# Four weight splits per LayerNorm moved from GpSimd to VectorE, and a constants step put on the background list

## Chip, cores, metric

One Trainium2 chip, one core. The metric is the device time of one launch in microseconds (us), the median of several runs; a profiled execution of the same program gives the trace.

## The reference, cut to what matters

Two layers of a trunk run over 640 tokens: a context part of 128 and a latent part of 512 tokens, 1024 features wide, in float32. Layer 0 has an even mixer (a gated MLP and pooling groups) and a convolutional feed-forward part; layer 1 has an odd mixer (a gated linear recurrence and latent attention) and another feed-forward part. Around each of the four sub-layers stand the same steps:

```python
sh1, sc1, g1, sh2, sc2, g2 = split(silu(c) @ w_mod[l] + b_mod[l], 6)   # one set for each of the two parts
h = x * (1 + sc) + sh
x = layernorm(ALPHA * x + g * sublayer(h)) * ln_g + ln_b
# feed-forward: z = dwconv3(h @ w_up); sublayer = (silu(z_gate) * z_value) @ w_down
# odd mixer, constants: -RG_C * softplus(-lam) for the decay of the recurrence
```

So w_mod (2 x 1024 x 6144) has to be multiplied by two vectors, once for each layer, and the gate g2 of layer 0 is needed when the first feed-forward's results are added up.

## The kernel before

**Products.** Each float32 product is made of three: a weight or an activation is split in a rounded part `hi` and a rest `lo`, and `mm3` (L150 to L155) runs hi x hi, hi x lo and lo x hi on TensorE. A weight's split (`split`, L96) is a cast on ScalarE (L98) and a subtraction (L101) on GpSimd or VectorE; `want` lists the weights in order of use with the engine for the subtraction (GpSimd where none is named). `load` (L115) issues a weight's DMA from SyncE into one of 4 raw buffers `r`, `prep` (L121) splits it into a pair of the 12 buffers `w`, `pump` (L136) keeps some weights loaded and split ahead, `take` hands one out.

**Order.** A scheduler orders the instructions of the engines by their place in the program and by modelled times; `high_priority` moves a split forward. `keep_in_program_order` pins an instruction behind the one that its engine was given just before in the program. The instructions of SyncE, that is all DMA issues, stay exactly in the order in which the program writes them.

**Sub-layers.** The 640 tokens are five tiles of 128 rows (`ys`). `project` (L474) makes the output product tile by tile in two halves of 512 columns, each in one of 4 PSUM buffers `B`; `accumulate` (L465) multiplies a half by the gate (L468, VectorE) and adds it to `ys` (L470 GpSimd, or L472 VectorE). In the last projection of a sub-layer `Norm` runs along: `stats` (mean, variance, L382 normalizes), `affine` (L403: scale L410, shift L413, of tiles 0 to 3), a shorter way for tile 4 (L370, then `second`, L392), and `turn` (L418), which transposes a normalized tile (L427) and splits it (L98, L101) into the next sub-layer's input. `project` ends with `turn(3)` and `turn(4)`, between them the first products of the next sub-layer (`nxt.start`), and sets `pin`, so that the next split alone is pinned.

**Feed-forward.** `ffn` goes over 22 column blocks p, each with a gate and a value product of 48 matmuls (PSUM buffers `A`, 2), a convolution (L527 ScalarE, L528 and L529 VectorE), and a product L538. They are grouped in pieces of 4, 4, 4, 3, 3 and 4 blocks (`PIECES`); after a piece is made, the piece before it is projected (`down`, which calls `project`).

**Background list.** `back` holds generators; `tick` runs the first one to its next `yield`, and the loops call it once or twice per product. `drain(k)` runs ticks until only k entries are left on the list. `mod_vec` (L250) is the modulation: for each of the 8 blocks of each of the vectors asked for it loads 512 KB of w_mod into a buffer `r` (L237, always one ahead) and multiplies it by the two vectors `cb` (L243, two VectorE instructions); after some vectors `rows_out` (L204) transposes the result on TensorE (L211), copies it (L213) and stores it to DRAM (`scr`, L215). `mod_bc` (L313) loads such rows back, spread over the partitions (L310).

After the even mixer the list holds the previous norm's `lazy` (L432), one vector of layer 0 (8 blocks) and five of layer 1 (40 blocks), written at the end as

```python
back.append(mod_vec(0, (5,), cb))
back.append(mod_vec(1, (0, 1, 2, 3, 4), cb))
rg_consts()
```

and in the feed-forward's `up`, after block p = 7, stands

```python
if p == PIECES[2] - 1:
    drain(1)
    gate.extend(mod_bc(l, SG2))
```

`rg_consts` (L934, through `softplus_neg`, L906) makes the odd mixer's constants with about 35 small VectorE instructions and one ScalarE instruction, from `vec`, which is loaded at the start.

Of the kernel before, what the change touches and what calls it, by code (L numbers as in the profile page):

```python
# [14 lines left out]
ALU = mybir.AluOpType  # L15
# [25 lines left out]
def tile_hybrid_trunk(ctx, tc, xT, x, vecs, tabs, wm0, wm1, wmT, crow, grow, lnrow, bs, w_u, w_v, w_p, w_s, w_pool, w_eo,  # L41
# [4 lines left out]
    dve, act, pe, pool, sp = nc.vector, nc.scalar, nc.tensor, nc.gpsimd, nc.sync  # L46
# [22 lines left out]
    def W(shape, dt=F32):  # L69
        return wpool.tile(shape, dt, tag="w", name=nm("w"))  # L70
# [4 lines left out]
    def Tm(shape, dt=F32):  # L75
        return tpool.tile(shape, dt, tag="t", name=nm("t"))

    def M(shape, dt=F32):
        return mpool.tile(shape, dt, tag="m", name=nm("m"))
# [10 lines left out]
    def B():  # L90
        return psB.tile([128, 512], F32, tag="B", name=nm("B"))
# [4 lines left out]
    def split(hi, lo, src, hi_eng, lo_eng):  # L96
        if hi_eng is act:
            act.copy(hi, src)  # L98
        else:
            hi_eng.tensor_copy(hi, src)  # L100
        return lo_eng.tensor_tensor(lo, src, f(hi), ALU.subtract)  # L101

# [1 line left out]
    queue = []  # L104
    ready = []
    loaded = []
    hold = [2]
    depth = [2]
    pin = [False]
    urgent = [True]  # L110

    def want(src, shape, scale=None, lo=None):
# [2 lines left out]
    def load():  # L115
        src, shape, scale, lo = queue.pop(0)
        raw = R(shape)
        sp.dma_start(raw, src)
        loaded.append((raw, shape, scale, lo))

    def prep(lo_eng=None):  # L121
        if not loaded:
            load()
        raw, shape, scale, lo_ = loaded.pop(0)
        lo_eng = lo_eng or lo_
        if scale is not None:
            dve.tensor_scalar(raw, raw, scale, ATTN_SCALE, ALU.mult, ALU.mult)
        hi, lo = W(shape, F32R), W(shape, F32R)
        with tc.high_priority() if urgent[0] else ExitStack():
            i = split(hi, lo, raw, act, lo_eng or pool)  # L130
        if pin[0]:
            tc.keep_in_program_order(i)
            pin[0] = False
        ready.append((hi, lo))

    def pump():  # L136
# [13 lines left out]
    def mm3(out, terms):  # L150
        n = len(terms)
        for i, (ah, al, bh, bl) in enumerate(terms):
            pe.matmul(out, ah, bh, start=i == 0, stop=False)  # L153
            pe.matmul(out, ah, bl, start=False, stop=False)  # L154
            pe.matmul(out, al, bh, start=False, stop=i == n - 1)  # L155
# [4 lines left out]
        pool.tensor_tensor(r, v, eps[:, 2:3], ALU.pow)  # L160
        return r

# [1 line left out]
    back = []  # L164

    def tick(n=1):
        for _ in range(n):
            while back:
                try:
                    next(back[0])  # L170
                    break
                except StopIteration:
                    back.pop(0)
# [2 lines left out]
        while len(back) > k:  # L176
            tick()

# [1 line left out]
    vec = cpool.tile([128, V_N], F32, name="vec")  # L180
    sp.dma_start(vec, vecs)
    ident = cpool.tile([128, 128], F32, name="ident")
# [9 lines left out]
    scr = [[dpool.tile([2, D], F32, name=f"scr{l}_{i}") for i in range(6)] for l in range(2)]  # L192
    SA1, SB1, SG1, SA2, SB2, SG2 = range(6)

# [1 line left out]
    def lnc(l, j):  # L196
        o = V_LN + (l * 4 + j) * 8
        return vec[:, o:o + 8].unsqueeze(1).to_broadcast([128, 2, 8])
# [117 lines left out]
    def ln_row(l, j):  # L316
        return bc_load(lnrow[:, (l * 4 + j) * D:(l * 4 + j + 1) * D])

# [1 line left out]
    def new_h():  # L320
        hi = [S([128, 2, T], F32R) for _ in range(4)]
        lo = [S([128, 2, T], F32R) for _ in range(4)]
        return hi, lo
# [14 lines left out]
        group(u, h, out, 0)  # L338
        group(u, h, out, 1)

# [1 line left out]
    ys = [None] * 5  # L342

    class Norm:
# [58 lines left out]
        def affine(self, i):  # L403
            y = ys[i]
            a, b = self.rows(i)
            ht = [Tm([128, 512]), Tm([128, 512])]
            for half in range(2):
                sl = slice(half * 512, half * 512 + 512)
                on_dve = half or self.nxt is None
                op = (dve if on_dve else pool).tensor_tensor(ht[half], y[:, sl], a[:, sl], ALU.mult)  # L410
                if on_dve:
                    tc.keep_in_program_order(op)
                (dve if half and (i == 3 or self.nxt is None or i == 0) else pool).tensor_tensor(ht[half], ht[half], b[:, sl], ALU.add)  # L413
                if self.nxt is None:
                    sp.dma_start(o_y[i][:, sl], ht[half])
            self.ht[i] = ht
# [42 lines left out]
    def settle():  # L459
        if pending[0] is not None:  # L460
            for _ in pending[0]:
                pass
            pending[0] = None
# [10 lines left out]
    def project(src, ks, wu, gate, norm=None, nxt=None, mid=None, ticks=1):  # L474
        settle()
        for i in range(5):
            c = slice(TOK[i], TOK[i] + 128)
            sums = None if norm is None else [M([128, 1]), M([128, 1])]
            for half in range(2):
                sl = slice(half * 512, half * 512 + 512)  # L480
                ps = B()
                mm3(ps, [(src[0][k // 2][:, k % 2, c], src[1][k // 2][:, k % 2, c], wu[n][0][:, sl], wu[n][1][:, sl])
                         for n, k in enumerate(ks)])
                accumulate(i, half, ps, gate, sums)
                if norm is not None and half == 0 and i and norm.fast(i - 1):
                    norm.second(i - 1)
            if mid is not None:
                mid(i)
            if norm is None:
                tick(ticks)  # L490
            else:
                norm.stats(i, sums, (lambda: norm.turn(i - 2)) if norm.nxt is not None and i >= 2 else None)
        if nxt is not None:
            next(nxt)
            norm.turn(3)
            next(nxt)
            norm.turn(4)
            pin[0] = True

# [1 line left out]
    def ffn(l, h):  # L501
        def plan():
            prev = None
# [124 lines left out]
                residual(norm)  # L628
        return nxt

# [1 line left out]
    def even_first(cb):  # L632
        want(w_v[0], [128, 2, 512])
        want(w_u[0], [128, D])
# [85 lines left out]
        for e in (dve, pool, dve):  # L720
            prep(e)
# [180 lines left out]
        nxt = out_proj(w_eo, ycat, gate, make_norm, nxt_sub, lambda i: pool_out(3, qs[3]) if i == 2 else None)  # L902
        return nxt, cb

# [1 line left out]
    def softplus_neg(lam):  # L906
        n = 8
        t, u, e, z, z2, s = (M([128, n]) for _ in range(6))
        dve.tensor_scalar(t, lam, -1.0, None, ALU.mult)
        dve.tensor_tensor(u, t, lam, ALU.max)  # L910
        act.activation(u, u, AF.Tanh, scale=1.0 / 32.0)
        dve.tensor_scalar(e, u, 1.0, None, ALU.add)
        dve.reciprocal(e, e)
        dve.tensor_scalar(u, u, -1.0, 1.0, ALU.mult, ALU.add)
        dve.tensor_tensor(e, e, u, ALU.mult)
        for _ in range(4):
            dve.tensor_tensor(e, e, e, ALU.mult)
        dve.tensor_scalar(z, e, 2.0, None, ALU.add)
        dve.reciprocal(z, z)
        dve.tensor_tensor(z, z, e, ALU.mult)  # L920
        dve.tensor_tensor(z2, z, z, ALU.mult)
        dve.tensor_scalar(s, z2, 1.0 / 17.0, 1.0 / 15.0, ALU.mult, ALU.add)
        for c in (13, 11, 9, 7, 5, 3, 1):
            dve.tensor_tensor(s, s, z2, ALU.mult)
            dve.tensor_scalar(s, s, 1.0 / c, None, ALU.add)
        dve.tensor_tensor(s, s, z, ALU.mult)
        dve.tensor_scalar(t, t, 0.0, None, ALU.max)
        dve.scalar_tensor_tensor(s, s, 2.0, t, ALU.mult, ALU.add)
        return s
# [2 lines left out]
    hb = cpool.tile([128, 16], F32, name="hb")  # L932

    def rg_consts():  # L934
        s = softplus_neg(vec[:, V_LAM:V_LAM + 8])
        dve.tensor_scalar(rg[:, 0:8], s, -2.0, None, ALU.mult)
        dve.tensor_scalar(rg[:, 8:16], s, -4.0, None, ALU.mult)
        dve.tensor_scalar(hb, vec[:, V_BA:V_BA + 16], 0.5, None, ALU.mult)

    def odd_mixer(h):  # L940
# [98 lines left out]
        def rest(make_norm, nxt_sub):  # L1039
# [166 lines left out]
                qt.append(q)  # L1206
            uk = take()

            # attention: heads in pairs
            kts = [[[W([96, 896], F32R) for _ in range(2)] for _ in range(1 + hh)] for hh in range(2)]  # L1210
            for kt, e in zip(kts[0] + kts[1], ((dve, act), (dve, act), (dve, act))):
                for q in range(2):
# [96 lines left out]
            for n in range(len(steps) + 3):  # L1309
                if n < len(steps):  # L1310
                    j, hh, i = steps[n]
# [23 lines left out]
                if n >= 3:  # L1335
                    j, hh, i = steps[n - 3]
# [29 lines left out]
        eng.tensor_tensor(x1, a, b, ALU.subtract)  # L1366
        eng.tensor_tensor(x2, c, e, ALU.add)

# [1 line left out]
    def sub(maker, *args):  # L1370
        return lambda h: Sub(*maker(*args, h))

    nxt, cb = even_mixer(lambda: Norm(0, 0, (0, SA2)), sub(ffn, 0))
    back.append(mod_vec(0, (5,), cb))
    back.append(mod_vec(1, (0, 1, 2, 3, 4), cb))
    rg_consts()
    nxt = nxt.rest(lambda: Norm(0, 2, (1, SA1)), sub(odd_mixer))
    nxt = nxt.rest(lambda: Norm(1, 0, (1, SA2)), sub(ffn, 1))
    cb = [V([128, D]) for _ in range(2)]
# [119 lines left out]
```

## Time and profile before

| | |
|---|---|
| time, median of 3 runs | 1579.65 us (1574.54 to 1591.32) |
| span of the profiled execution | 1581.2 us |
| TensorE busy in it | 1473.5 us (93%) |
| VectorE, GpSimd, ScalarE busy | 1002.7, 785.0 and 585.9 us |
| mean granted TensorE clock | 0.976 |

The times are those of the launch; of the profiled execution the span from its first to its last instruction is given, and no other time of its own. The span stands 1.6 us above the median and inside the three runs. Busy times of different engines lie beside each other; TensorE's idle time is what an improvement elsewhere can take away.

### The profile page before, as it was taken

To read this page: it belongs to the slowest core of one execution; us is meant where nothing else is said; L and a number is where in the kernel's file an instruction comes from. 1 tells how busy PE (TensorE), PEld (TensorE's weight loads), DVE (VectorE), ACT (ScalarE), POOL (GpSimd) and SP (SyncE) were. 2 spreads that over 40 slices of the span, in tenths; PEclk is the share of its full clock that TensorE was granted. 3 is DMA by queue.
4 is the path that set the end of the run, shared out by engine and by line. 5 is a ranking of instruction groups with operands and counts; after the bars stand their busy time and mean duration, and the time that the engine had idled before them with its cause. 6 is when DMAs were issued, how large, how long until landed. Compare 5 with 4: busy or idle time off the path is not lost. (4 is left out here: it accounts for less than half of the span.)

```text
span 1581.2 us, 21997 instructions
## 1 busy us (share of the span) xinstructions
PE 1473.5 (93%) x8741; PEld 1320.6 (84%) x8741; DVE 1002.7 (63%) x1432; ACT 585.9 (37%) x868; POOL 785.0 (50%) x564
## 2 busy tenths in 40 slices
PE   6889988899799999899979899998999999999997
PEld 3675868898799898887969788777999898999995
DVE  3485686577976778648688667858585342423347
ACT  3422354231323132324566465625334232322323
POOL 1132476634746466547367410576538816255444
PEclk9999999999999999999999899999999999999999
DMA  9345613243444353421220100352342421221311
GB/s 380 130 160 200 253 43 104 80 134 134 166 153 148 119 175 120 136 105 60 98 87 1 57 1 1 121 189 78 120 133 107 134 81 57 91 80 54 94 41 67
DMA packets 51734, 177.61 MB, mean 112 GB/s; under 512 B 6128, under 2 KB 6704, under 8 KB 51632
## 3 DMA queue, kind: packets, MB, share of 16 engines
q1 hardware_dynamic: 51632, 176.21, 32.6%
q8 instruction: 69, 1.13, 0.3%
q14 instruction: 33, 0.27, 0.1%
HBM read 170.71 MB, written 5.48 MB: 111 GB/s over the span
## 5 line engine op out<-in xcount | busy, mean ns | idle before, releaser
L101 POOL TENSOR_TENSOR w<-r,w 128x1024 fp32r<-128x1024 f32 (+2 forms) x148 | 369.8, 2508 | 465.6 <-ACT w L98 453.6
L153 PE MATMUL A<-s,w 128*128 128x258 f32 (+1 forms) x1672 | 525.9, 315 | 28.8 <-DVE t L529 19.2
L154 PE MATMUL A<-s,w 128*128 128x258 f32 (+1 forms) x1672 | 524.6, 314 | 3.8 <-DVE s L101 3.8
L155 PE MATMUL A<-s,w 128*128 128x258 f32 (+1 forms) x1672 | 523.9, 314 | 0.6 <-POOL w L101 0.6
L153 PEld LDWEIGHTS A<-s,w 128*128 128x128 f32 x1672 | 320.7, 192 | 41.0 <-issue 30.5
L98 ACT CAST w<-r 128x1024 fp32r<-128x1024 f32 (+3 forms) x184 | 186.6, 1029 | 389.1 <-PE B L154 168.3
L154 PEld LDWEIGHTS A<-s,w 128*128 128x128 f32 x1672 | 321.5, 192 | 7.7 <-DVE s L101 4.6
L155 PEld LDWEIGHTS A<-s,w 128*128 128x128 f32 x1672 | 320.8, 192 | 3.4 <-issue 2.5
L154 PE MATMUL B<-w,s 128*128 128x512 f32 (+2 forms) x734 | 283.2, 386 | 6.6 <-DVE w L101 6.6
L153 PE MATMUL B<-w,s 128*128 128x512 f32 (+2 forms) x734 | 283.5, 387 | 0.0
L155 PE MATMUL B<-w,s 128*128 128x512 f32 (+2 forms) x734 | 282.2, 384 | 0.0
L470 POOL TENSOR_TENSOR y<-y,t 128x512 f32<-128x512 f32 x120 | 183.0, 1537 | 112.9 <-DVE t L468 103.1
L528 DVE SCALAR_TENSOR_TENSOR t<-A,vec,t 128x641 f32<-128x641 f32 x88 | 77.7, 883 | 215.1 <-ACT t L527 210.2
L468 DVE TENSOR_TENSOR t<-B,s 128x512 f32<-128x512 f32 x160 | 108.7, 686 | 125.6 <-PE B L155 107.6
L243 DVE SCALAR_TENSOR_TENSOR t<-r,v 128x1024 bf16<-128x1024 f32 x112 | 185.2, 1658 | 2.9 <-DMA r<-in_wmT_dram 2.2
L154 PEld LDWEIGHTS B<-w,s 128*128 128x128 f32 x734 | 139.0, 189 | 34.4 <-DVE w L101 8.0
L155 PEld LDWEIGHTS B<-w,s 128*128 128x128 f32 x734 | 139.1, 190 | 27.4
L153 PEld LDWEIGHTS B<-w,s 128*128 128x128 f32 x734 | 139.1, 190 | 27.0 <-DVE t L468 0.2
L98 ACT CAST s<-t 128x642 fp32r<-128x642 f32 x60 | 43.8, 730 | 199.8 <-DVE t L538 166.9
L101 DVE TENSOR_TENSOR w<-r,w 128x1024 fp32r<-128x1024 f32 (+2 forms) x36 | 56.5, 1577 | 50.3 <-ACT w L98 50.2
L529 DVE SCALAR_TENSOR_TENSOR t<-A,vec,t 128x641 f32<-128x641 f32 x88 | 77.8, 885 | 2.7
L527 ACT ACTIVATE t<-A,vec 128x642 f32<-128x642 f32 x88 | 77.5, 881 | 5.0 <-PE A L155 4.5
(249 smaller groups left out, 1602.3 us busy)
## 6 DMA issues: line engine op xcount, KB each, us to landing
r<-in_w_up_dram SPq DMA_DIRECT2D x88, 512.0 KB, 3.6
r<-in_wmT_dram SPq DMA_DIRECT2D x56, 512.0 KB, 3.2
r<-in_w_dn_dram SPq DMA_DIRECT2D x44, 512.0 KB, 3.6
s<-scr SPq DMA_DIRECT2D x20, 512.0 KB, 6.6
s<-in_wm_dram SPq DMA_DIRECT2D x16, 512.0 KB, 9.3
r<-in_wm_dram SPq DMA_DIRECT2D x16, 512.0 KB, 4.4
s<-in_wmT_dram SPq DMA_DIRECT2D x8, 512.0 KB, 3.4
r<-in_w_eo_dram SPq DMA_DIRECT2D x8, 512.0 KB, 4.2
```

The lines of the kernel that those rows point to most:

```text
L98: act.copy(hi, src)
L101: return lo_eng.tensor_tensor(lo, src, f(hi), ALU.subtract)
L153: pe.matmul(out, ah, bh, start=i == 0, stop=False)
L154: pe.matmul(out, ah, bl, start=False, stop=False)
L155: pe.matmul(out, al, bh, start=False, stop=i == n - 1)
L243: op = dve.scalar_tensor_tensor(junk, raw, 1.0, cb[s], ALU.mult, ALU.mult, accum_out=mc[l][:, m, s, k:k + 1])
L468: dve.tensor_tensor(t, ps, gate[stream(i)][:, sl], ALU.mult)
L470: pool.tensor_tensor(ys[i][:, sl], ys[i][:, sl], t, ALU.add)
L527: act.activation(t, z, AF.Identity, bias=cb, scale=w1)
L528: dve.scalar_tensor_tensor(t[:, 1:], z[:, :T - 1], w0, t[:, 1:], ALU.mult, ALU.add)
L529: dve.scalar_tensor_tensor(t[:, :T - 1], z[:, 1:], w2, t[:, :T - 1], ALU.mult, ALU.add)
```

## The change

Four edits:

1. `project` no longer sets a flag that pins the next split; it calls `prep(dve, True)` four times after `turn(4)`, so that the subtractions of the next four weights are VectorE's, each pinned behind what VectorE was given before it.
2. `affine` of tile 3 is all VectorE's: the first half's scale and shift leave GpSimd.
3. `rg_consts` is a generator and goes on the background list behind the two `mod_vec` entries, instead of running at once; it yields once before it does anything.
4. The first instruction of `softplus_neg` is pinned in program order.

The last norm (`nxt is None`) is not touched by the first two. Lines that only change a comment are left out of the diff.

```diff
-    pin = [False]
...
-    def prep(lo_eng=None):
+    def prep(lo_eng=None, pin=False):
...
             i = split(hi, lo, raw, act, lo_eng or pool)
-        if pin[0]:
+        if pin:
             tc.keep_in_program_order(i)
-            pin[0] = False
...
-                on_dve = half or self.nxt is None
+                on_dve = half or i == 3 or self.nxt is None
                 op = (dve if on_dve else pool).tensor_tensor(ht[half], y[:, sl], a[:, sl], ALU.mult)
                 if on_dve:
                     tc.keep_in_program_order(op)
-                (dve if half and (i == 3 or self.nxt is None or i == 0) else pool).tensor_tensor(ht[half], ht[half], b[:, sl], ALU.add)
+                (dve if i == 3 or half and (self.nxt is None or i == 0) else pool).tensor_tensor(ht[half], ht[half], b[:, sl], ALU.add)
...
             norm.turn(4)
-            pin[0] = True
-
+            for _ in range(4):
+                prep(dve, True)
...
-        dve.tensor_scalar(t, lam, -1.0, None, ALU.mult)
+        tc.keep_in_program_order(dve.tensor_scalar(t, lam, -1.0, None, ALU.mult))
...
     def rg_consts():
+        yield
         s = softplus_neg(vec[:, V_LAM:V_LAM + 8])
...
     back.append(mod_vec(1, (0, 1, 2, 3, 4), cb))
-    rg_consts()
+    back.append(rg_consts())
```

## Rows read from the trace of the kernel before

**Rows 1.** The page's first part: busy us (share of the span), instructions.

```profile
PE 1473.5 (93%) x8741; PEld 1320.6 (84%) x8741; DVE 1002.7 (63%) x1432; ACT 585.9 (37%) x868; POOL 785.0 (50%) x564
```

**Rows 2.** Windows at the first LayerNorm's end: busy us by engine, clock, DMA.

```profile
235.00:242.00 7.00, 1.35 (x7) 0.83 (x7) 6.93 (x9) 1.88 (x7) 5.61 (x3) 0.71 0.63 209
242.00:249.00 7.00, 7.00 (x33) 7.00 (x34) 5.55 (x31) 2.02 (x4) 0.33 (x1) 0.80 0.56 210
```

**Rows 3.** Timeline of TensorE there: start, us, line; idle before it in brackets.

```profile
241.89 0.69 PE L154 MATMUL A<-s,w 128*128 128x384 f32 x1 [3.83 <-DVE s L101]
```

**Rows 4.** Timeline of VectorE there.

```profile
229.65 0.74 DVE L370 SCALAR_TENSOR_TENSOR t<-y,m,s 128x512 f32<-128x512 f32 x1
...
230.64 5.46 DVE L392 SCALAR_TENSOR_TENSOR t<-t,m,s 128x512 f32<-128x512 f32 x2
...
236.36 1.99 DVE L909 TENSOR_SCALAR m<-vec 128x8 f32<-128x8 f32 x1
...
240.67 0.17 DVE L927 TENSOR_SCALAR m<-m 128x8 f32<-128x8 f32 x1
240.75 2.40 DVE L101 TENSOR_TENSOR s<-B,s 128x256 fp32r<-128x256 f32 x7
...
249.41 0.89 DVE L528 SCALAR_TENSOR_TENSOR t<-A,vec,t 128x641 f32<-128x641 f32 x1 [1.01 <-ACT t L527]
```

**Rows 5.** Timeline of GpSimd there.

```profile
230.39 10.22 POOL L101 TENSOR_TENSOR w<-r,w 128x1024 fp32r<-128x1024 f32 x4
```

**Rows 6.** Timeline of SyncE's DMA issues after block 7 of the first feed-forward.

```profile
370.65 0.33 SPq L215 DMA_DIRECT2D scr<-t  x1
371.08 0.36 SPq L237 DMA_DIRECT2D r<-in_wmT_dram  x1
372.01 0.80 SPq L310 DMA_DIRECT2D s<-scr  x2
372.91 0.85 SPq L118 DMA_DIRECT2D r<-in_w_up_dram  x2
```

**Rows 7.** Line L243 alone, 380 to 645 us: duration ns min/median/max, first and last start.

```profile
L243 DVE SCALAR_TENSOR_TENSOR t<-r,v x80: 1212/1402/3432, 380.0 to 640.8; 128x1024 bf16<-128x1024 f32 x80
```

**Rows 8.** Waits of TensorE, 398 to 652 us: total us, times, longest.

```profile
PE A L153 <- DVE t L529: 13.4, 7, 4.7
```

**Rows 9.** The page's fifth part: busy us, mean ns, idle before and releaser.

```profile
L528 DVE SCALAR_TENSOR_TENSOR t<-A,vec,t 128x641 f32<-128x641 f32 x88 | 77.7, 883 | 215.1 <-ACT t L527 210.2
...
L101 DVE TENSOR_TENSOR w<-r,w 128x1024 fp32r<-128x1024 f32 (+2 forms) x36 | 56.5, 1577 | 50.3 <-ACT w L98 50.2
```

**Rows 10.** Timeline of VectorE at the second and the third LayerNorm's end.

```profile
748.49 4.36 DVE L392 SCALAR_TENSOR_TENSOR t<-t,m,s 128x512 f32<-128x512 f32 x2
...
1105.47 5.45 DVE L392 SCALAR_TENSOR_TENSOR t<-t,m,s 128x512 f32<-128x512 f32 x2
```

**Rows 11.** The page's sixth part: DMA issues, KB each, median us to landing.

```profile
r<-in_wmT_dram SPq DMA_DIRECT2D x56, 512.0 KB, 3.2
...
s<-scr SPq DMA_DIRECT2D x20, 512.0 KB, 6.6
```

**Rows 12.** Timeline of VectorE where two L243 follow each other, near 641 us.

```profile
640.85 1.23 DVE L243 SCALAR_TENSOR_TENSOR t<-r,v 128x1024 bf16<-128x1024 f32 x1
...
642.12 2.23 DVE L248 TENSOR_TENSOR mc<-mc,vec 128x16 f32<-128x16 f32 x1
```

**Rows 13.** Timeline of VectorE: the first accumulation after block 7.

```profile
378.81 1.29 DVE L468 TENSOR_TENSOR t<-B,s 128x512 f32<-128x512 f32 x2 [8.80 <-PE B L155]
```

**Rows 14.** Timeline of TensorE around that projection.

```profile
372.96 0.39 PE L153 MATMUL B<-w,s 128*128 128x512 f32 x1
...
398.07 0.28 PE L154 MATMUL A<-s,w 128*128 128x258 f32 x1
...
408.11 0.36 PE L153 MATMUL A<-s,w 128*128 128x258 f32 x1 [4.69 <-DVE t L529]
```

**Rows 15.** Line L243 as a group, 370 to 652 us: busy us, mean ns.

```profile
L243 DVE SCALAR_TENSOR_TENSOR t<-r,v 128x1024 bf16<-128x1024 f32 x80 | 136.3, 1707 | 2.8 <-DMA r<-in_wmT_dram 2.2
```

## Prediction

> **What bounds the kernel now.** I read the page's busy times first. TensorE is busy for 1473.5 of 1581.2 us [rows 1], so 107.7 us of idle time is all that anything outside its own work can give back, while anything that holds its inputs adds time in full. Then I looked where that idle time lies, in windows of 20 us, and took two places that the change touches.
>
> The first is the end of a LayerNorm. In the 7 us from 235 TensorE works for 1.35 us, and in the next 7 its clock is 0.80 [rows 2]; its longest wait there is 3.83 us, for a split by VectorE [rows 3]. VectorE's own rows say why: the two L392 take 5.46 us, though a like instruction (L370, same shape) takes 0.74, and then the odd constants stand ahead of the last seven splits, from 236.36 to 240.75 [rows 4]. While both are slow, GpSimd runs four weight splits without a break, 10.22 us from 230.39 [rows 5]. This is what edits 1, 3 and 4 aim at.
>
> The second is in the first feed-forward after block 7, where the list is emptied down to one entry. SyncE's issues are seen in written order: store of the finished vector's row, one modulation load, the two loads of the gate, two weights [rows 6]. So of the 40 blocks of layer 1 only the first is asked for here. The rest is spread by ticks: 80 L243, from 380.0 to 640.8 us [rows 7], in the shade of TensorE's work. What of it shows is some waiting of TensorE for the convolution: 13.4 us in 398 to 652 [rows 8].
>
> **The change part by part.**
>
> *Splits and affine (edits 1, 2), three LayerNorms.* GpSimd's four splits leave the stretch of L392. At 0.74 each the two cost 1.48: 5.46 - 1.48 = 4.0 us earlier at the first norm [rows 4], 2.9 at the second and 4.0 at the third [rows 10]. Added ahead of them on VectorE are a scale and a shift of 128x512, at some 0.74 to 1 us each: 1.7 us. Net 2.3, 1.2 and 2.3 us. The four weight splits themselves go to VectorE at 1.58 us [rows 9], 6.3 us behind the last split of the tile. What they would hold up is the next convolution on VectorE; between the last split's end (243.15) and that convolution at 249.41 [rows 4] lie 6.3 us, filled now by small constants. So I cost them at nothing; without that cover they cost up to 6.3 us at each norm, 19 in all. The first of them is needed only after both starting products have run. Casts stay on ScalarE. The loads of two of the four weights move in SyncE's queue ahead of what follows the norm (lazy's rows; in the odd mixer the five spills); the raw buffers come free by the same splits, some us later or earlier, and I cost this at nothing between -2 and +3 us.
>
> *Constants moved (edits 3, 4).* 4.4 us leave the first norm's path [rows 4]. They come back as 35 small instructions near 0.17 us [rows 4], 6 us, in a tick of the projection behind the pin, beside TensorE's work; bounds 0 to 6.
>
> With the clock's loss after the wait (7 us at 0.80, 1.4 us [rows 2]) the norms give 2.3 + 4.4 + 1.4 + 1.2 + 2.3, about 12 us; bounds 0 (the splits hold the convolutions) and 20.
>
> *The list has one entry more.* This is the large term. `drain(1)` stops with one entry left. Before, that entry is layer 1's `mod_vec`; now it is `rg_consts`, so all 40 blocks, with their loads, their 80 L243 and three `rows_out`, are run at that point of the program. In SyncE's order 39 more loads and five stores stand ahead of the gate's two loads, and with 4 raw buffers the loads go only as fast as VectorE frees them. Every accumulation of the projection that follows reads the gate. Behind the gate stand the next weights.
>
> The time, step by step. The first load is issued at 371.08 [rows 6] and lands 3.2 us later [rows 11]: 374.3. An L243 takes 1.21 us at best [rows 7], 1.23 with 1.27 to the next instruction in [rows 12]; GpSimd has nothing to do in this stretch, so I take 1.26: 80 x 1.26 = 100.8. Some 22 small instructions at 0.17 [rows 4] make 3.7. Twice SyncE waits for a row to store before it may issue the next load, and the loads need 3.2 us again; with the two convolutions of block 8 (four at 0.88 [rows 9] and their ends) I set 6 us, between 2 and 10. That makes 484.8. From the last copy to the gate's issue: 0.8 (transpose, copy, store) + 0.8 (two stores, at 0.33 to 0.4 us [rows 6]). From the issue at 372.01 [rows 6] to the first accumulation at 378.81 [rows 13] are 6.8 us, beside a median of 6.6 to landing [rows 11]. The first accumulation is then at 493.2 instead of 378.81, 114.4 us later. The row names TensorE for that wait, but its first half was done by 373 [rows 14], so it was the gate.
>
> What TensorE has to do meanwhile: four halves, one for each buffer B, and the rest of block 8's value product, which before ran from 398.07 [rows 14] to 403.43. Nine halves run from 372.96 to 398.07, 2.79 us each. Before, from the first accumulation to block 9 (408.11) it takes 29.3 us. Now six halves are left, 16.7 us, with 0.7 for the first accumulation and 3 for a clock that a long idle time leaves at its lower level: 20.4. So 8.9 us come back, and the stop costs 114.4 - 8.9 = 105.5 us.
>
> *After it* no modulation runs beside the feed-forward. Of the 13.4 us [rows 8] 4.7 belong to the wait before block 9 [rows 14], already counted; of the other 8.7, and the waits for two later rows, I take 9; bounds 2 and 13.
>
> Sum: +105.5 - 12 - 9 = +84.5 us. On the median, 1579.65, that is **1664 us**; on the profiled span, 1581.2, 1666.
>
> *The price of L243.* The rows hold two: 1.21 us at best and 3.43 at worst [rows 7], with a mean of 1.707 where GpSimd splits weights and adds beside it [rows 15]. By the mean the 80 would take 136.6 us, 35.8 more than my sum. I take the lower price, since GpSimd's next work waits for the accumulations.
>
> The Trainium skill, GPSIMD Engine Reference, Specifications, says that GpSimd shares its SBUF interfaces with VectorE and contends with VectorE instructions that have two SBUF inputs. By that rule the lower price holds with GpSimd idle, and the sum is the one above; if GpSimd worked throughout, it would be 1700. The two L392 beside GpSimd's splits [rows 4, 5] agree with it.
>
> **Rivals.**
>
> *Only the norms show (faster).* If TensorE's work covers the emptied list, 12 + 9 us are left: 1559. It decides so if at least 114 us of products can run without the gate and without new weights. Against it: four halves and one part of a product, 16 us, are all that has buffers and weights. 4%.
>
> *A longer stop.* GpSimd or the DMAs slow L243, or only two of the four raw buffers turn over: then a block takes (3.2 + 0.4 + 2.5)/2 = 3.05 us and 40 take 21 us more. 1685, and 1700 by the mean of [rows 15]. For it: rows at 3.4 us. Against: three loads into raw buffers are issued within 2 us there [rows 6], so at least three are free at that time. 15%.
>
> *A shorter stop.* The scheduler finds more to run ahead, the norms and the later feed-forward give their upper bounds (20 and 13): 1664 - 12 - 8 = 1644, less if the convolutions and row waits cost 2. 13%.
>
> *The splits hold the convolutions.* 19 us at the norms: 1683 with the stop. 5%.
>
> **How the numbers follow.** The forecast's own case, 1650 to 1680, has 63%. Reaching to the longer and the shorter stop the range is 1640 to 1698. About 1% (16 us) is what a measurement can tell from no change, since the three runs lie 17 us apart. Faster by over 1%: 4%, from the first rival. Within 1%: 2%, if half of the stop is covered and the rest is given back. Slower by over 1%: 94%.
>
> **What would show it.** In the trace after: all 80 L243 of layer 1 in some 110 us after block 7, at 1.2 to 1.3 us each; SyncE issuing 39 modulation loads in a row ahead of the gate's two; TensorE and GpSimd idle for about 100 us, in one piece, ended by a DMA of the gate through L468; no L243 from about 490 to the feed-forward's end. At the norms: L392 at 0.74, no L909 near 236, TensorE's 3.83 us wait gone, L101 on VectorE for weights right behind the last tile's splits. Wrong would be: gate loads issued early, L243 still spread over the feed-forward, or L392 still at 2.7 us.

## The result, and the profile after

The changed kernel takes 1657.89 us (median; four runs, 1649.97 to 1667.52). Against the kernel before, run beside it, the ratio is 1.0497, with a 95% interval of 1.0456 to 1.0538. The forecast of 1664 is a ratio of 1.0534; the range held. The profiled run took 1649.97 us, with a span of 1647.8, 66.6 more than the span before. In the changed kernel most line numbers are two less: L243, the multiplication of a block of w_mod by one vector, is L241, and L468 is L466. One such multiplication adds up its products, and is called a sum below.

The experiments were made in four sets on three chips, each set with the kernel before beside it (medians 1575.21, 1578.2, 1575.79 and 1577.86 us), so between sets the ratios are compared first. One of the six runs of e10, 2441.91 us at a granted clock of 0.557 where the other five have 0.948 to 0.950, is a slow run and not in its ratio.

The page's first part, beside [rows 1]: no engine does more than before, and GpSimd is busy for 64 us less; TensorE merely stands longer.

```profile
PE 1465.9 (89%) x8741; PEld 1315.3 (80%) x8741; DVE 965.0 (59%) x1451; ACT 585.7 (36%) x868; POOL 720.8 (44%) x545
```

SyncE's timeline after block 7, beside [rows 6]: start, length, line. Three gaps stand between the loads of the sums, where the next store waits for a row; the gate's two loads (L308) come last.

```profile
352.65 0.32 SPq L213 DMA_DIRECT2D scr<-t  x1
353.08 35.27 SPq L235 DMA_DIRECT2D r<-in_wmT_dram  x17
397.19 0.79 SPq L213 DMA_DIRECT2D scr<-t  x2
398.08 14.07 SPq L235 DMA_DIRECT2D r<-in_wmT_dram  x8
420.20 0.33 SPq L213 DMA_DIRECT2D scr<-t  x1
420.62 31.12 SPq L235 DMA_DIRECT2D r<-in_wmT_dram  x15
463.00 0.79 SPq L213 DMA_DIRECT2D scr<-t  x2
463.83 0.90 SPq L308 DMA_DIRECT2D s<-scr  x2
```

TensorE's timeline there, only instructions that follow an idle time, beside [rows 14]. The stop is in three pieces, each ended by a row transpose (L209) that waited for VectorE's copy of the sums, not by the gate. The last row is block 9.

```profile
396.43 0.39 PE L209 MATMUL B<-ident,m 128*32 128x128 f32 x1 [38.90 <-DVE m L206]
419.50 0.38 PE L209 MATMUL B<-ident,m 128*16 128x128 f32 x1 [22.68 <-DVE m L206]
462.29 0.40 PE L209 MATMUL B<-ident,m 128*32 128x128 f32 x1 [42.41 <-DVE m L206]
...
496.07 0.36 PE L151 MATMUL A<-s,w 128*128 128x258 f32 x1 [3.43 <-DVE t L528]
```

The line of the sums from 350 to 462 us, beside [rows 7]: one sum ahead of the stop and all 80 of layer 1, at a median of 1.224 us, with hardly any spread.

```profile
L241 DVE SCALAR_TENSOR_TENSOR t<-r,v x81: 1212/1224/1227, 349.7 to 459.8; 128x1024 bf16<-128x1024 f32 x81
...
  DMA r<-in_wmT_dram: 10.3, 3
```

VectorE's first accumulation, beside [rows 13], and the first convolution of block 8 that follows the projection:

```profile
467.95 0.69 DVE L466 TENSOR_TENSOR t<-B,s 128x512 f32<-128x512 f32 x1 [5.71 <-DMA s<-scr]
...
494.12 0.89 DVE L527 SCALAR_TENSOR_TENSOR t<-A,vec,t 128x641 f32<-128x641 f32 x1 [0.68 <-ACT t L526]
```

Windows of the stop and behind it (busy us by engine, clock, DMA): GpSimd does nothing in the 104 us, the granted clock is 0.52 in them, nearly all at its lower level of 1.2 GHz, and 0.59 in the 6 us that follow, 2.5 us lost.

```profile
358.00:462.00 104.00, 0.78 (x2) 0.19 (x2) 96.28 (x175) 0.51 (x2) 0.00 (x0) 0.52 0.57 188
462.00:468.00 6.00, 5.71 (x16) 4.53 (x17) 0.25 (x3) 0.25 (x1) 0.00 (x0) 0.59 0.48 161
```

The first LayerNorm, on VectorE, beside [rows 4]: the two second scales (now L390) take 1.41 us, no constants stand behind them, and the weight splits leave room for the convolutions (L527).

```profile
231.28 1.41 DVE L390 SCALAR_TENSOR_TENSOR t<-t,m,s 128x512 f32<-128x512 f32 x2
232.60 1.41 DVE L101 TENSOR_TENSOR s<-B,s 128x256 fp32r<-128x256 f32 x4
...
236.04 3.49 DVE L101 TENSOR_TENSOR w<-r,w 128x1024 fp32r<-128x1024 f32 x3
239.44 0.88 DVE L527 SCALAR_TENSOR_TENSOR t<-A,vec,t 128x641 f32<-128x641 f32 x1
240.24 1.22 DVE L101 TENSOR_TENSOR w<-r,w 128x1024 fp32r<-128x1024 f32 x1
```

The two windows of [rows 2], after: TensorE's clock is at its upper level and it hardly stops.

```profile
235.00:242.00 7.00, 7.00 (x41) 6.76 (x39) 6.56 (x8) 4.98 (x6) 0.00 (x0) 1.00 0.43 141
242.00:249.00 7.00, 6.68 (x46) 6.63 (x46) 3.71 (x5) 4.82 (x6) 4.76 (x2) 1.00 0.98 346
```

Put together from such rows, the two profiled executions differ so (the landmarks: the store behind block 7, block 9, the second scales of norms 2 and 3, the end):

| stretch | before | after | difference | forecast |
|---|---|---|---|---|
| start to store behind block 7 | 370.65 | 352.65 | -18.0 | -8.1 |
| store to block 9 | 37.46 | 143.42 | +106.0 | +105.5 |
| block 9 to norm 2 | 340.38 | 322.08 | -18.3 | -9 |
| norm 2 to norm 3 | 356.98 | 357.32 | +0.3 | -1.2 |
| norm 3 to end | 475.73 | 472.33 | -3.4 | -2.3 |
| sum | 1581.2 | 1647.8 | +66.6 | +84.9 |

(The forecast's 84.9 is the recorded 84.5 with the norms' terms, 11.6, not rounded to 12.) The stop is as forecast to half a microsecond. Both gains ahead of it and behind it are twice the forecast. On the medians the difference is 78: the profiled run of after is the lowest of its four, 7.9 below their median, the span before stands 1.6 above its median, and a time is 2.2 longer than its span (1649.97 and 1647.8).

### The profile page after: what moved, and what is told of

It reads as the page before. It is cut to its first block, busy times and chain, and to the rows that moved or that the text cites. A ratio compares the mean times of both kernels' runs of the same rounds, so it can differ in the third digit from the quotient of the medians.

```text
span 1647.8 us, 21998 instructions
## 1 busy us (share of the span) xinstructions
PE 1465.9 (89%) x8741; PEld 1315.3 (80%) x8741; DVE 965.0 (59%) x1451; ACT 585.7 (36%) x868; POOL 720.8 (44%) x545
## 5 line engine op out<-in xcount | busy, mean ns | idle before, releaser
L101 POOL TENSOR_TENSOR w<-r,w 128x1024 fp32r<-128x1024 f32 (+3 forms) x136 | 331.9, 2451 | 474.0 <-ACT w L98 473.9
L151 PEld LDWEIGHTS A<-s,w 128*128 128x128 f32 x1672 | 316.8, 190 | 21.4 <-issue 9.6
L152 PEld LDWEIGHTS A<-s,w 128*128 128x128 f32 x1672 | 317.4, 190 | 3.6 <-issue 2.5
L153 PEld LDWEIGHTS A<-s,w 128*128 128x128 f32 x1672 | 317.0, 190 | 3.9 <-issue 2.5
L468 POOL TENSOR_TENSOR y<-y,t 128x512 f32<-128x512 f32 x120 | 165.3, 1383 | 223.7 <-DVE t L466 209.1
L527 DVE SCALAR_TENSOR_TENSOR t<-A,vec,t 128x641 f32<-128x641 f32 x88 | 77.8, 884 | 268.4 <-ACT t L526 268.3
L466 DVE TENSOR_TENSOR t<-B,s 128x512 f32<-128x512 f32 x160 | 109.5, 688 | 159.9 <-PE B L153 133.1
L241 DVE SCALAR_TENSOR_TENSOR t<-r,v 128x1024 bf16<-128x1024 f32 x112 | 142.6, 1296 | 11.8 <-DMA r<-in_wmT_dram 10.3
L101 DVE TENSOR_TENSOR w<-r,w 128x1024 fp32r<-128x1024 f32 (+3 forms) x48 | 68.3, 1438 | 52.1 <-ACT w L98 52.0
L209 PE MATMUL B<-ident,m 128*16 128x128 f32 (+1 forms) x7 | 2.3, 324 | 105.9 <-DVE m L206 105.9
L209 PEld LDWEIGHTS B<-ident,m 128*16 128x16 f32 (+1 forms) x7 | 0.6, 93 | 107.2 <-DVE m L206 107.2
```

What stands on the lines that cost most here:

```text
L209: pe.transpose(ps[:16 * n, :128], col.rearrange("p n s k -> p (n s k)"), ident)
L241: op = dve.scalar_tensor_tensor(junk, raw, 1.0, cb[s], ALU.mult, ALU.mult, accum_out=mc[l][:, m, s, k:k + 1])
L466: dve.tensor_tensor(t, ps, gate[stream(i)][:, sl], ALU.mult)
L468: pool.tensor_tensor(ys[i][:, sl], ys[i][:, sl], t, ALU.add)
L527: dve.scalar_tensor_tensor(t[:, 1:], z[:, :T - 1], w0, t[:, 1:], ALU.mult, ALU.add)
```

## The experiments

**The stop: e2, e5, e4, e10.** Four kernels ask what it consists of. The first is the kernel before with only the list's part of the change (edits 3 and 4: the constants become a list entry):

```diff
-    rg_consts()
+    back.append(rg_consts())
```

> The kernel before with edits 3 and 4 alone: the constants wait on the background list, the splits and the affine stay as they were. Theory 1, the emptied list: the stop after block 7 comes from the list's extra entry alone, so it is here in full, about 106 us between the store of the row and block 9, less 4 us at the first norm and 9 to 18 us in the later feed-forward: 1660 to 1675 us. Rival, the stop needs the moved splits (raw buffers or VectorE's order changed by edits 1 and 2): within 10 us of the kernel before, 1570 to 1590.

1674.75 us, ratio 1.0631 (1.0601 to 1.0662). In the trace the store is at 372.22 and block 9 follows 143.21 us later, as in the changed kernel (143.42). The whole stop comes from the list's one entry more. Block 9 on TensorE's timeline:

```profile
515.43 0.56 PE L153 MATMUL A<-s,w 128*128 128x258 f32 x1 [3.42 <-DVE t L529]
```

In e5 each sum of layer 1 in the changed kernel reads 512 of its 1024 columns, so half of each sum is left out:

```diff
-            op = dve.scalar_tensor_tensor(junk, raw, 1.0, cb[s], ALU.mult, ALU.mult, accum_out=mc[l][:, m, s, k:k + 1])
+            w = 512 if l == 1 else D
+            op = dve.scalar_tensor_tensor(junk[:, :w], raw[:, :w], 1.0, cb[s][:, :w], ALU.mult, ALU.mult, accum_out=mc[l][:, m, s, k:k + 1])
```

> The changed kernel, but the two instructions of L241 read 512 of the 1024 columns for layer 1 (half of each sum is left out); all loads keep their 512 KB. Theory 1, VectorE paces the emptied list at 1.26 us an instruction: 80 instructions fall to about 0.7 to 0.75 us, the stop is some 40 us shorter, 1615 to 1625 us. Rival, the loads pace it (2.5 us for a load of 512 KB is their rate): the stop stays near 105 us, 1650 to 1665, with VectorE idle for about half of it and waiting for DMAs.

1619.55 us, 38 below the changed kernel's median, or 34 by the ratios (1.0281 and 1.0497); the span is 30.5 shorter, the three gaps 72.0 us instead of 104.0. A sum takes 0.691 us, which over 80 is 42.6 saved; 6.6 of them went back into waits for the loads (16.9 instead of 10.3) that the sums had covered. VectorE sets the length of the stop, with the loads close behind it. The rival's 2.5 us is not the rate of a load: in e5 the 40 loads are issued from 353.22 to 423.17, 1.75 us each on average. The line of the sums in e5:

```profile
L242 DVE SCALAR_TENSOR_TENSOR t<-r,v x81: 684/691/1210, 349.9 to 428.5; 128x512 bf16<-128x512 f32 x80, 128x1024 bf16<-128x1024 f32 x1
...
  DMA r<-in_wmT_dram: 16.9, 13
```

In e4 the gate is loaded ahead of the emptying, not behind it:

```diff
-                    drain(1)
+                    drain(2 if l == 0 else 1)
                     gate.extend(mod_bc(l, SG2))
+                    drain(1)
```

> The changed kernel, but at block 7 the list is emptied to two entries, then the gate's two loads are issued, then it is emptied to one: the same 40 blocks at the same place of the program, only the gate's loads stand ahead of them in SyncE's order. Theory 1, the gate's place in SyncE's queue: the gate lands some 7 us after block 7, the projection of 28 us runs inside the stop, and what is left waits for the weights of block 9: 20 to 28 us shorter, 1630 to 1640 us. Rival A, VectorE's order (80 pinned L241 ahead of the accumulations hold them): as the changed kernel, 1650 to 1665, with the gate landed early and the first accumulation still after the last L241. Rival B, the PSUM buffers or TensorE's order (the halves stand behind the row transposes): also 1650 to 1665, with no half computed before the last row transpose.

1660.58 us (1654.71 and 1666.45), ratio 1.0541 (1.045 to 1.0633): nothing is gained, and theory 1 falls. SyncE issues the gate's loads 110 us earlier, yet the first accumulation on VectorE comes at 470.23, and it waits for TensorE, which has done no half before the last row transpose at 465.41. SyncE's timeline in e4, then VectorE's:

```profile
353.64 0.80 SPq L308 DMA_DIRECT2D s<-scr  x2
```

```profile
470.23 0.69 DVE L466 TENSOR_TENSOR t<-B,s 128x512 f32<-128x512 f32 x1 [4.88 <-PE B L153]
```

So e10 left the gate behind and moved something else: the row transposes of layer 1, with their stores, come behind the first down projection (their columns have tiles of their own, so that they last until then):

```diff
+        def send():
+            ps = B()
+            pe.transpose(ps[:16 * n, :128], col.rearrange("p n s k -> p (n s k)"), ident)
...
+        if l == 1 and items[0][0] != SG2:
+            late.append(send)
+        else:
+            send()
...
                     down(*prev)
+                    while late:
+                        late.pop(0)()
```

> The changed kernel, with the four row transposes of layer 1 and their stores moved behind the first down projection; the sums on VectorE and their place stay. Theory 1, that the projection's first four halves did not run inside the stop because in TensorE's own stream they stand behind the row transposes, which wait for the last sums: now four halves run right behind block 7, the three gaps become one, and the time is 8 to 12 below the changed kernel (1645 to 1651 against 1657.9). Rival: they wait for the gate or for VectorE's order; nothing changes, 1655 to 1660.

1639.84 us (five of the six runs within 1638.59 and 1640.35), 18 below the changed kernel's median, where 8 to 12 were expected, and 14 by the ratios (1.0408 and 1.0497); span to span, which compares two executions without the hold-up told of below, 11.1. Now the projection's first halves run in the first 12 us of what was the stop, and one gap is left, which an accumulation ends that frees a buffer B. Windows of e10, then SyncE's, VectorE's and TensorE's timelines:

```profile
358.00:370.00 12.00, 10.11 (x54) 8.86 (x52) 11.83 (x21) 0.00 (x0) 0.00 (x0) 1.00 0.73 244
370.00:452.00 82.00, 0.00 (x0) 0.00 (x0) 80.58 (x146) 0.00 (x0) 0.00 (x0) 0.51 0.68 219
```

```profile
352.52 92.53 SPq L243 DMA_DIRECT2D r<-in_wmT_dram  x40
445.10 0.90 SPq L316 DMA_DIRECT2D s<-scr  x2
```

```profile
453.00 0.69 DVE L474 TENSOR_TENSOR t<-B,s 128x512 f32<-128x512 f32 x1
...
478.27 0.89 DVE L535 SCALAR_TENSOR_TENSOR t<-A,vec,t 128x641 f32<-128x641 f32 x1 [1.74 <-ACT t L534]
```

```profile
453.74 0.80 PE L151 MATMUL B<-w,s 128*128 128x512 f32 x1 [85.63 <-DVE t L474]
...
481.32 0.55 PE L151 MATMUL A<-s,w 128*128 128x258 f32 x1 [5.04 <-DVE t L536]
```

In the changed kernel the transposes stood ahead of the projection's halves in TensorE's order, and waited for the sums. Block 9 comes 129.23 us after the store (352.09), 14.2 earlier than in the changed kernel. All of that lies ahead of the first accumulation, which comes 100.9 us after the store, not 115.3; from there to block 9 it takes 28.3 us, as in the changed kernel (28.1), though four halves are done. The edit does two things: the halves no longer stand behind the transposes, and SyncE no longer waits for rows, so that the gate's loads are issued 93.0 us after the store, not 111.2. The gate's place alone is worth nothing (e4); whether the halves' place alone is worth all of it, no run tells.

**What the rest is worth: e1, e6, e3, e7.** With the list emptied to two entries in the first feed-forward the stop is gone. e1 is the changed kernel with that alone:

```diff
-                    drain(1)
+                    drain(2 if l == 0 else 1)
```

> The changed kernel with the list emptied to two entries after block 7 of layer 0, so that the modulation is spread again; all else as changed. Theory 1, the list's extra entry is the whole loss: the stop is gone and the norms' gain is left, 18 us up to block 7 and 3 at the third norm by the trace, so 1555 to 1565 us, faster than before by 1 to 1.6%. Rival, part of the loss is elsewhere (pinned splits holding convolutions): 1575 us or more.

1566.1 us, ratio 0.9923 (0.9896 to 0.995), twelve runs from 1556.93 to 1578.86: 12 us less than before, and 1 above the upper end of what was expected. Then its parts, on the kernel before. e6 has edit 1 alone (`pin` is gone, and `for _ in range(4): prep(dve, True)` stands behind the last tile), e3 edits 1 and 2, e7 the constants as a list entry with that same `drain(2 ...)`, and nothing else.

> The kernel before with edit 1 alone, without the fourth tile's affine on VectorE. My reckoning has the affine add 1.7 us to VectorE's chain at each norm: then this is 3 to 5 us faster than edits 1 and 2 together. Rival, GpSimd's 2.6 us for the half are longer than VectorE's 1.4: 0 to 5 us slower than both together. Either way 1563 to 1577 us.

> The kernel before with edits 1 and 2 alone: four splits and the fourth tile's affine on VectorE, the constants stay at once and unpinned. If the splits free L392 (4.0, 2.9 and 4.0 us, less 1.7 for the affine) and the constants' 4.4 us stay on the first norm's path: 1570 to 1575 us. If most of the 18 us up to block 7 comes from GpSimd being free for the lazy rows earlier, and not from the norm's own chain: 1560 to 1566, as the version with the list mended.

> The kernel before with edits 3 and 4 alone and the list emptied to two entries after block 7. By the norm's chain 4.4 us leave it: 1573 to 1577 us. Rival, the constants only fill VectorE's waiting beside GpSimd's splits there and taking them away gives nothing: 1579 to 1582.

e6: 1566.49, ratio 0.9948 (0.9915 to 0.9982). e3: 1584.17, ratio 1.0027 (1.0006 to 1.0047), a clear miss: no gain. e7: 1569.55, below the 1573 to 1577 expected, but ratio 0.9974 (0.9938 to 1.001), with eight runs from 1567.3 to 1570.3 and four from 1581 to 1590. None of these is the sum of the norms' terms, so I looked for another loss, and found one behind the first norm that the prediction has no word of. In the kernel before, VectorE and GpSimd (two timelines):

```profile
284.26 11.48 DVE L538 TENSOR_TENSOR t<-t,t 128x642 f32<-128x642 f32 x1
```

```profile
278.46 11.87 POOL L449 TENSOR_TENSOR y<-y,s 128x1024 f32<-128x1024 f32 x5
290.29 4.77 POOL L101 TENSOR_TENSOR w<-r,w 128x1024 fp32r<-128x1024 f32 x2
```

A product of 128x642 that elsewhere takes 0.82 us takes 11.48, until GpSimd's unbroken run ends. TensorE waits for the convolution queued behind it, and then has a clock of 0.55 for 7 us (its timeline, then a window, both of the kernel before):

```profile
300.22 0.55 PE L153 MATMUL A<-s,w 128*128 128x258 f32 x1 [5.40 <-DVE t L529]
```

```profile
300.00:307.00 7.00, 6.78 (x31) 6.81 (x32) 3.50 (x5) 3.19 (x4) 2.38 (x1) 0.55 0.44 144
```

By an estimate from these rows that costs 5.40 and 7 x 0.45 = 3.2, near 9 us. In e6 it is worse: the product takes 20.45 us, beside the last nine of eleven GpSimd operations (VectorE's and GpSimd's timelines).

```profile
264.56 20.45 DVE L537 TENSOR_TENSOR t<-t,t 128x642 f32<-128x642 f32 x1
```

```profile
258.53 11.89 POOL L447 TENSOR_TENSOR y<-y,s 128x1024 f32<-128x1024 f32 x5
270.38 2.40 POOL L101 TENSOR_TENSOR w<-r,w 128x1024 fp32r<-128x1024 f32 x1
272.75 11.57 POOL L447 TENSOR_TENSOR y<-y,s 128x1024 f32<-128x1024 f32 x5
```

In e3 it hits the constants: with edits 1 and 2 and without edits 3 and 4 eight of these 128x8 operations, 0.17 us each otherwise, fall beside GpSimd's run and take 2.26 to 2.32, one GpSimd operation each, with a convolution queued behind them. TensorE waits 16.9 us, and e3's gain is gone (VectorE's timeline of e3, then TensorE's waits from 240 to 320 us).

```profile
252.18 2.29 DVE L924 TENSOR_SCALAR m<-m 128x8 f32<-128x8 f32 x1
254.51 2.32 DVE L923 TENSOR_TENSOR m<-m,m 128x8 f32<-128x8 f32 x1
...
268.34 2.26 DVE L923 TENSOR_TENSOR m<-m,m 128x8 f32<-128x8 f32 x1
```

```profile
PE A L151 <- DVE t L528: 17.2, 2, 16.9
```

TensorE's longest wait at this place is 5.4 us before, 14.3 in e6, 16.9 in e3, 11.1 in e1, 13.2 in e2; in the changed kernel, in e4, e5 and e10, which are the changed kernel up to the stop, and in e7 the same product takes 2.93 at most, and no wait is over 0.4. The length varies from kernel to kernel and, to judge by the two clusters of e7's runs, from execution to execution.

Two pairs of traces show what the hold-up costs. Up to the store behind block 7, e1 is the same program as the changed kernel; e1 has the hold-up, and its store comes at 366.79 instead of 352.65, 14.1 us later. In the same way e2 is e7 up to there: 372.22 with the hold-up (19.26 us), 356.58 without. SyncE's timelines of e1 and of e7:

```profile
366.79 0.33 SPq L213 DMA_DIRECT2D scr<-t  x1
```

```profile
356.58 0.32 SPq L215 DMA_DIRECT2D scr<-t  x1
```

**Is it the hold-up: e8, e9, e11, e12.** The ten operations (scale and shift of y, L449) go from GpSimd to VectorE, in the kernel before (e8), in e1 (e9), and in e1 without edit 2 (e11); e12 is e1 without edit 2, with them on GpSimd.

```diff
-                    pool.tensor_tensor(ys[i][:, sl], ys[i][:, sl], parts[q], ALU.add if q >= n else ALU.mult)
+                    (dve if (self.l, self.j) == (0, 0) else pool).tensor_tensor(ys[i][:, sl], ys[i][:, sl], parts[q], ALU.add if q >= n else ALU.mult)
```

> The kernel before, with one thing moved: the ten full-row operations that scale and shift y behind the first norm (the line y<-y,s, 2.4 us each on GpSimd, run back to back in the first feed-forward) go to VectorE. Theory 1, that a VectorE product of two tiles in local memory can be held up behind these back-to-back GpSimd operations (11.48 us in the trace before, 20.45 us with the splits alone, against 0.82 us) and that TensorE then stands still 5 to 17 us: no VectorE instruction over 3 us between 245 and 300, no TensorE gap over 3 us between 250 and 310, a median 5 to 12 below the kernel before (1566 to 1573), and runs that lie within some 6 us of each other where those before spread over 14. Theory 2, that the gap is VectorE's own load at that place: ten more operations there make it longer, 1580 to 1590.

> The changed kernel with the list left as it was before (emptied only down to two entries in the first feed-forward) and with those ten operations on VectorE. Theory 1: the hold-up of 11.06 us in the trace of the same kernel with them on GpSimd is gone; median 1548 to 1558 against 1566, and the spread of the runs halves. Theory 2 (VectorE's load): 1566 or above.

> As e9_best, but the fourth tile's affine is left as it was before (three of its four operations, GpSimd doing the first half). By the prediction's price (1.7 us per norm, twice or three times) it is the same as e9_best or up to 5 us slower. By the rival, that more work on VectorE beside the norms costs as much as it saves: 0 to 5 us faster than e9_best.

> The changed kernel with the list left as it was before (two entries left in the first feed-forward) and with the fourth tile's affine left as it was before: edits 1 and 4 at work, edit 2 not, and the ten operations on y back on GpSimd. Against the same with edit 2 (1566.1, runs of 1556.93 to 1578.86) it tells what edit 2 is worth, against the same with the ten operations on VectorE (1562.1, runs within 5.6) what these cost there. Theory A, that edit 2 adds work to VectorE for nothing, since the splits' move alone brings the second scale from 2.7 to 0.74 us: 1556 to 1562. Theory B, that edit 2 costs only beside the ten operations on VectorE: 1565 to 1568. If the hold-up of a VectorE product beside GpSimd's run of ten operations comes in some executions and not in others, the runs spread over 10 to 20 us in either case.

| kernel | median us | runs | ratio, interval | longest wait, 240 to 320 |
|---|---|---|---|---|
| e8 | 1577.41 | 1573.53 to 1580.98 | 1.0013 (0.9999 to 1.0026) | 3.8 |
| e9 | 1570.13 | 1566.73 to 1575.09 | 0.9962 (0.9945 to 0.9979) | 2.5 |
| e11 | 1562.11 | 1558.26 to 1563.84 | 0.9911 (0.9893 to 0.993) | 0.2 |
| e12 | 1571.87 | 1558.59 to 1581.36 | 0.9951 (0.9919 to 0.9983) | 13.1 |

The mechanism came out as theory 1 has it: no instruction of VectorE there is over 3.5 us, the hold-up's wait is gone in all three (e8's 3.8 is that of [rows 3], at the norm). The spread is 8 us in e9 and 6 in e11, against 22 in e1 and 23 in e12, but that doesn't show it: e9 and e11 ran on another chip than e1 and e12, and there the kernel before, which has the hold-up in its trace, spreads over 9 us, on the other two chips over 14 and 15. The gain did not follow in every kernel: e8's and e9's medians miss what was expected, and by the ratios e9 (0.9962) is no faster than e1 (0.9923). In e8 the store behind block 7 is 7.0 us earlier, at 363.64, but from there to norm 2 it takes 3.8 us more, and its median is that of before: what was gained is lost again, probably to the ten more operations on VectorE, which no run shows apart. e11 has the lowest ratio of all kernels, 0.9% below before, but e1's interval covers it. What edit 2 is worth beside GpSimd's run e12 doesn't tell: its median lies outside what either theory expected, and its runs and e1's overlap over 20 us. With the ten operations on VectorE, the affine on VectorE costs 8.0 us (e9 against e11, 0 to 5 expected). Between the two traces it is 5.0, of which 6.6 lie between norm 1 and norm 2 and -1.6 elsewhere; what it is made of stays open.

## Why the prediction was right

**The stop** (+105.5, measured +106.0) is right as a sum and partly by luck. The first sum starts 3.7 us after the store, as worked out. A sum takes 1.224 us, 97.8 for 80 instead of 100.8, and the last ends at 461.0, so the list takes 104.7 us from the landing where I had 110.5. From there to the first accumulation are 7.0 us (8.4 forecast). So this is 107.1 us later than before, not 114.4. Against that, the credit of 8.9 us failed: I let four halves and the rest of block 8's value product run during the stop. None did. From the first accumulation to block 9 it took 28.1 us, against 29.3 before, and the convolutions of block 8 came at 494. Nor would the halves alone have brought the credit: in e10, where they did run, it is 28.3. There the six halves left end 20.8 us after the first accumulation, as the 20.4 had it, but the convolutions of block 8 stand behind the last accumulations (478.27), with the moved transposes between, and block 9 waits for them; the 29.3 held such a wait of 4.69 [rows 14], and the 20.4 left it out. The reason I had given for the order, that accumulations wait for the gate, is what released the first accumulation (467.95), but the halves held it as long: the first of them could begin only at 462.3, behind the last transpose. e4 brought the gate forward and gained nothing, e10 took the transposes and the rows' stores away and got back 11.1 of span, ahead of the first accumulation. "In one piece, ended by the gate" was wrong too: three pieces, ended by the transposes. The clock's loss behind it, 2.5 us, was set at 3.

**The price of a sum** was the right one of two: with GpSimd at 0.00 us busy in the 104 us, all 80 take the lower price. The rule I took from the Trainium skill's GPSIMD Engine Reference, Specifications, agrees with that, as do the tensor_tensor rows of e3 and e6.

**The norms** (-12, of them -8.1 at the first). At the first norm the steps came out: second scales from 5.46 to 1.41, constants gone, VectorE's last tile split done at 236.1 instead of 243.15, which is 7.0 against 2.3 + 4.4; the wait of 3.83 gone, the clock back from 0.80 to 1.00. The four weight splits cost nothing, as I had it: one of them even ran behind the convolution, and TensorE waited 0.7 us in all from 240 to 350. The affine, set at 1.7 us, delayed the second scales by 0.64. But edit 2 wasn't needed for them: with edit 1 alone (e6) they take 1.40 us. What the term left out is the hold-up of 11.48 us at 284.26 and the clock behind it, near 9 us of the span before, which this execution of the changed kernel doesn't have: 8.1 + 9 is 17.1 of the 18.0. The pairs above bear it out: 14.1 and 15.6 us for hold-ups of 16.90 and 19.26. It is a mis-sized term by omission: I had read the waits at the norm's end and not those 50 us behind it, though GpSimd's earlier freedom moves the ten operations that stand there. That this execution has none is luck as far as the prediction goes. The other runs of the changed kernel, 1662.82 and 1667.52, may have the hold-up, as e1 does, but they have no traces. Norm 3 gave 3.4 for 2.3 and norm 2 nothing for 1.2.

**Later feed-forward** (-9, measured -18.3). I priced TensorE's waits alone. From 409 to 743 us they are, before (what is waited for: total us, times, longest):

```profile
PE A L153 <- DVE t L529: 8.8, 6, 2.6
PE B L211 <- DVE m L208: 3.7, 3, 1.8
PE B L427 <- POOL t L413: 0.9, 1, 0.9
```

After, from 497 to 813, only the last of these is left. So 12.5 us of waits go. Some of the remaining 5.8 lies in TensorE's busy time, 320.68 us in the one stretch against 315.08 in the other, at a clock of 0.99 and 1.00: the waits seem to cost clock too, as at the norm.

**The rivals.** Neither the longer stop (the sums did not slow) nor the splits that hold the convolutions came. The shorter stop named the right error, gains at their upper bounds of 20 and 13: the stretches gave 21.1 and 18.3, the first of them only through the hold-up.

## What to carry to other kernels

A count that says how far a list is emptied depends on everything that is ever put on the list: one entry more at its end moved 80 sums, 39 loads and three transposes into one place, for 106 us. What ran during this stop was decided by each engine's own order, so ask for every engine which waiting instruction stands first, not only which transfer comes late. And where two execution times of one kernel differ by more than the effect that is looked for, look in the trace for an instruction that is far longer than its like, before the parts are priced.

## What the runs showed of the hardware

A VectorE operation on tiles in local memory beside an unbroken run of GpSimd's two-input operations can take one GpSimd operation's time (2.26 to 2.32 us for 128x8, 0.17 alone) or that of many (11.48, 16.90, 19.20, 19.26 and 20.45 us for a product of 0.82): until the run ended, and in e1 (16.90) until the ninth of the ten operations on y did. Also the second scale (L390) came down from 2.7 and 2.8 to 0.74 us when only GpSimd's splits were moved away (e6). The Trainium skill, SBUF — State Buffer, "SBUF: two separate sides", calls the port pair that the two engines share an exclusive lock, which the first to start holds for its whole instruction. The rows of 2.3 us agree; the 20.45 us goes on over several GpSimd instructions (nine of the eleven in e6's rows, the third already under way), so here VectorE did not get its turn when one ended. Why it does at some of them (2.89 us in the changed kernel, beside the same run) and not at others, no run here shows.
